# The first weight blocks of v and the second token tile: one load each instead of two

## The chip, the cores and the metric

The kernel runs on one NeuronCore of one Trainium2 chip. The metric is device time in microseconds (us), the median over several executions. An execution that is taken by the hardware profiler gives the trace and the page of the profile; it has a time of its own.

A core has five engines that run side by side, each through its own list of instructions in order: PE (TensorE, matrix products), DVE (VectorE), ACT (ScalarE), POOL (GpSimd) and SP (SyncE, which here only issues transfers). Transfers between HBM and the core's own memory run on 16 DMA engines, which take what SP and ACT issue.

## The reference

One layer of a bidirectional encoder on 1024 tokens of width 1024, all in float32:

```python
h = layer_norm(x, emb_ln_g, emb_ln_b)               # embedding LayerNorm
proj = h @ w_in                                     # 1024 x 5120
q, k, v, z_a, u, z_b, g_a, g_b = split(proj)        # widths 512 x6, 1024 x2
attn = neighbourhood_attention(q, k, v, rpb)        # 8 heads x 64, 8x16 window on a 16x64 grid
y_a = attn * silu(z_a)
u = centred_depthwise_conv(u, conv_w, conv_b)
h2 = rg_lru(u, forward) + rg_lru(u, backward)       # scans along the sequence
y_b = h2 * silu(z_b)
m = sigmoid(g_a + b0) * (y_a @ w_ba) + sigmoid(g_b + b1) * (y_b @ w_bb)
out = layer_norm(ALPHA * h + m @ w_out, ln_g, ln_b)
```

The part that the change touches is the very start: the embedding LayerNorm of the first tokens, and v = h @ w_v, where w_v is 1024 x 512.

## The kernel before

**Tiles.** The 1024 tokens are eight tiles x0 to x7 of 128 tokens x 1024 values (512 KB each). A tile is normalised with the tokens on the 128 partitions, then PE turns it around in two halves of 512 features (`turn(i, kk)`), since a product needs the features on the partitions. w_v is cut into eight blocks k = 0 to 7 of 128 x 512 (256 KB each); they lie in HBM in four pairs c = 0 to 3, and in a pair the two blocks of a partition are side by side, 4 KB in all.

**High and low parts.** For float32 accuracy each operand is split into a rounded high part and a low part (the value less its high part), and a product is three matmuls: high x high, low x high, high x low. For a weight block, ACT makes the high part (`wv_hi(k)`, line 203) and POOL then the low part (`wv_lo(k)`, line 206, recorded at the helper's line 134). For a turned half tile ACT makes the high part (line 368; for the first half of x0 line 514) and DVE the low one (also line 134). `v_part(i, kind, ks)` (line 413) issues the matmuls of tile i: kind "h" needs the high parts of the blocks ks, "a" the low part of the tokens, "w" the low part of the weights.

**The order.** What each engine does, and in which order, is written out by hand from line 487 on, and each engine goes through its list in order. At the start:

- SP issues x0 (two halves), block 0, block 1, pair 1, x1 (two halves), pairs 2 and 3, x2, the first weights of q, x3, x4, some small values, xt4, and then stores the normalised x0 to HBM (`keep(0)`, line 270). Pairs 0 and 1 go to the tile `wvsh`, pairs 2 and 3 to `wvsl`.
- ACT: root for x0, high parts of blocks 0 and 1, high part of the first turned half of x0 (line 514), high parts of blocks 2 and 3, of the second turned half (line 368), of blocks 4 and 5, root for x1 (line 236), high parts of blocks 6 and 7, and so on.
- POOL: the low parts of blocks 0 to 7, one after the other.
- DVE: statistics of x0 and its normalisation, low part of its first turned half, statistics of x1 (line 230, two instructions, one for each half), low part of the second turned half of x0, normalisation of x1 (lines 251, 244 to 246, 254).
- PE: warm-up products on zeros, spreading of gain and bias, first half of x0 turned (line 359), v of x0 with blocks 0 and 1, second half of x0 turned, then the rest of v of x0 as the blocks come, x1 turned, v of x1, and so on. A matmul of v that needs block 4 is the first that needs pair 2.

**Counters of the loads.** Each transfer is booked on one of eight counters, DMAHW0 to DMAHW7, in turn. A transfer is issued only when the transfer eight places before it, which used the same counter, has landed.

**Later.** The token tile x5 uses the memory of x0, so its load waits until the store of x0 has landed; in the same way x6 waits for the store of x1. Around 30 us the results v of the first tiles are stored (`v_d`, line 427), and the buffer `vs` of such a result is written again (line 420) only when the store has landed. At 47.67 us PE spreads the statistics of x7 (`bcp`, line 323), which takes what ACT and DVE have done until then.

Of the kernel before, what the change touches and what calls it, by code (L numbers as in the profile page):

```python
# [72 lines left out]
def encoder_kernel(ctx, tc, x, xt, gb1, gb, w_qk, w_v, w_s, w_ba, w_bb, w_gate, smalls, bias, w_out, out):  # L73
    nc = tc.nc
    V, A, G, PE, SP = nc.vector, nc.scalar, nc.gpsimd, nc.tensor, nc.sync
# [86 lines left out]
    wvs = [hts[0].tile([P, 4, HALF], F32, tag="ht4" + c, name=f"wvs{c}") for c in "hl"]  # L162
# [25 lines left out]

    def load_x(i):
        xs[i] = ln.tile([P, D], F32, tag="x", bufs=5, name=f"x{i}")  # L190
        if i < 2:
            for sl in halves:
                SP.dma_start(xs[i][:, sl], x[i][:, sl])
        else:
            SP.dma_start(xs[i][:], x[i])

    def load_wv(c):
        for part in ((0,), (1,)) if c == 0 else ((0, 1),):
            k = 2 * (c % 2) + part[0]
            SP.dma_start(wvs[c // 2][:, k:k + len(part), :], w_v[c][:, part[0]:part[-1] + 1])  # L200

    def wv_hi(k):
        A.copy(wv[0][k][:], wvs[k // 4][:, k % 4, :])  # L203
# [282 lines left out]

    A.dma_start(gb_row[:], gb1.rearrange("o z (r f) -> (o z r) f", f=P))
    load_x(0)
    load_wv(0)
    load_wv(1)  # L490
    load_x(1)
    load_wv(2)
    load_wv(3)
    load_x(2)
    qk_load(0)
    load_x(3)
# [665 lines left out]
    for slot in range(7 * N_PAIR + 4):  # L1162
        p, k = divmod(slot, 7)
# [184 lines left out]
    for unit in range(-NT, H * NT + PV_LAG):  # L1348
        h, c = divmod(unit, NT)
# [538 lines left out]
```

## Time and profile before

| what | value |
|---|---|
| median of 3 runs | 657.51 us (657.47 to 657.64) |
| profiled execution: its time | 658.84 us |
| profiled execution: its span, first to last instruction | 657.1 us |
| PE busy | 644.1 us, 98% of the span |
| DVE, ACT, POOL busy | 540.6, 413.5, 399.2 us |
| transfers | 118.66 MB, 181 GB/s in the mean |

The span is what the page describes; 1.7 us of the profiled execution's time lie outside it, and it is 1.3 us longer than the median of the plain runs. In the views, a line of the timeline gives start, duration, engine, line of the kernel, operation and what is written and read; in brackets stands how long the engine was idle before, and what ended that. "SPq" is SP's issue of a transfer, and the time beside it is that of issuing, not of moving the data. L140, L134 and the like are lines of the kernel; a helper's line stands for all its callers.

### The profile page before, as it was taken

The page shows a single profiled execution, that of the slowest core. Times are in us where ns is not written, and L with a number is a line of the kernel's source. Part 1 is how long each engine was busy: PE and PEld are TensorE (multiplying, and loading weights), DVE is VectorE, ACT ScalarE, POOL GpSimd, SP SyncE. Part 2 cuts the span into 40 slices and gives each one's busy share as a digit, 9 for nine tenths or more (in the row PEclk, how much of TensorE's full clock was granted, in tenths as well). Part 3 has the DMA queues.
Part 4 walks back from the last instruction along what each step waited for, and adds up shares of the span by engine and source line. Part 5 has one row for each costly group of instructions (what it writes and reads, how often), then busy time and mean ns, then how long its engine had stood idle before and what let it go on. Part 6 is the DMA issues. An engine that isn't in the chain of part 4 may idle for free.

```text
span 657.1 us, 9482 instructions
## 1 busy us (share of the span) xinstructions
PE 644.1 (98%) x3089; PEld 539.4 (82%) x3089; DVE 540.6 (82%) x849; ACT 413.5 (63%) x738; POOL 399.2 (61%) x326
## 2 busy tenths in 40 slices
PE   7999999999999999999999999999999999999994
PEld 6888888888878888888888888889888888888884
DVE  7988998995999799979988695277887875994776
ACT  5569554567776677777666745277777744574253
POOL 5559769933655576558556434012652649989957
PEclk9999999999999999999999999999999999999998
DMA  8674676433333233532362548797977288333033
GB/s 327 218 288 149 197 238 252 145 128 113 128 102 118 87 113 119 170 113 80 135 217 67 186 174 303 280 351 261 359 277 244 66 314 291 111 116 129 17 112 129
DMA packets 54065, 118.66 MB, mean 181 GB/s; under 512 B 5680, under 2 KB 10368, under 8 KB 52480
## 3 DMA queue, kind: packets, MB, share of 16 engines
q1 hardware_dynamic: 53696, 117.67, 51.9%
q8 instruction: 24, 0.39, 0.2%
q10 hardware_dynamic: 320, 0.40, 0.2%
q14 instruction: 25, 0.20, 0.1%
HBM read 82.36 MB, written 35.68 MB: 180 GB/s over the span
## 4 chain that ended last, share of the span: by engine, by line
PE 86%; DVE 6%; DMA 3%; ACT 2%; issue 1%; SPq 0%; DVEq 0%; ACTq 0%
PE a L140 32%; PE mb L140 13%; PE s L140 12%; PE x L140 6%; PE w L140 5%; PE v L413 4%; PE acc L1267 3%; PE s L1219 3%; PE pt L1241 3%; PE g L885 2%; PE q L140 2%; DMA v_d<-vs 1%; DMA wvsl<-in_w_v_dram 1%; DVE uc L843 1%; DVE ws_l L134 1%
## 5 line engine op out<-in xcount | busy, mean ns | idle before, releaser
L140 PE MATMUL a<-ht_h,ws_h 128*128 128x512 f32 x136 | 53.0, 389 | 0.0
L140 PE MATMUL a<-ht_h,ws_l 128*128 128x512 f32 x136 | 52.9, 389 | 0.0
L140 PE MATMUL a<-b_h,wa_h 128*128 128x512 f32 x136 | 52.9, 389 | 0.0
L140 PE MATMUL a<-b_h,wa_l 128*128 128x512 f32 x136 | 52.9, 389 | 0.0
L140 PE MATMUL a<-ht_l,ws_h 128*128 128x512 f32 x136 | 52.9, 389 | 0.0
L140 PE MATMUL a<-b_l,wa_h 128*128 128x512 f32 x136 | 52.9, 389 | 0.0
L1229 DVE CUSTOM_DVE_ANT_0 sc<-s,bias 128x384 f32<-128x384 f32 (+1 forms) x64 | 33.4, 522 | 19.8 <-PE s L1219 9.8
L1248 ACT CAST pt_h<-pt 128x384 fp32r<-128x384 f32 x64 | 29.0, 453 | 23.1 <-PE pt L1241 18.9
L993 POOL CAST wb_h<-wb 128x512 fp32r<-128x512 f32 x9 | 7.0, 781 | 58.3 <-DMA wb<-in_w_bb_dram 37.4
L1234 ACT ACTIVATE p<-sc,summ 128x384 f32<-128x384 f32 (+1 forms) x64 | 37.8, 591 | 5.5 <-DVE summ L1229 5.2
L140 PE MATMUL mb<-ya,wb_h 128*128 128x512 f32 x128 | 39.6, 389 | 0.0
L134 DVE TENSOR_TENSOR pt_l<-pt,pt_h 128x384 fp32r<-128x384 f32 x64 | 33.2, 519 | 1.8 <-ACT pt_h L1248 1.5
L413 PE MATMUL v<-wv,b_h 128*128 128x512 f32 x128 | 32.7, 397 | 1.1 <-ACT wv L203 0.7
L1219 PE MATMUL s<-ks,qs 128*128 128x384 f32 (+1 forms) x128 | 31.7, 329 | 0.0
L1642 POOL TENSOR_TENSOR z<-z,gb 128x512 f32<-128x512 f32 (+1 forms) x22 | 25.9, 1189 | 9.0 <-ACT z L1637 8.2
L1241 PEld LDWEIGHTS pt<-ident,p 128*128 128x128 f32 x176 | 22.9, 140 | 8.9 <-issue 0.9
L140 PEld LDWEIGHTS a<-ht_h,ws_h 128*128 128x128 f32 x136 | 25.5, 188 | 5.5 <-issue 0.2
L140 PEld LDWEIGHTS a<-ht_l,ws_h 128*128 128x128 f32 x136 | 25.5, 188 | 5.3
L140 PEld LDWEIGHTS a<-b_l,wa_h 128*128 128x128 f32 x136 | 25.5, 188 | 5.3
L140 PEld LDWEIGHTS a<-b_h,wa_l 128*128 128x128 f32 x136 | 25.5, 188 | 5.3
L140 PEld LDWEIGHTS a<-b_h,wa_h 128*128 128x128 f32 x136 | 25.5, 188 | 5.3
L140 PEld LDWEIGHTS a<-ht_h,ws_l 128*128 128x128 f32 x136 | 25.5, 188 | 5.2
(579 smaller groups left out, 2296.6 us busy)
## 6 DMA issues: line engine op xcount, KB each, us to landing
ks<-k_d SPq DMA_DIRECT2D x8, 1024.0 KB, 7.5
v_d<-vs SPq DMA_DIRECT2D x8, 512.0 KB, 3.3
q_d<-q SPq DMA_DIRECT2D x8, 512.0 KB, 3.0
ga_d<-ga SPq DMA_DIRECT2D x16, 256.0 KB, 2.0
gb_d<-gb SPq DMA_DIRECT2D x16, 256.0 KB, 2.7
k_d<-k SPq DMA_DIRECT2D x8, 512.0 KB, 3.5
qs<-q_d SPq DMA_DIRECT2D x8, 512.0 KB, 6.0
g<-gb_d SPq DMA_DIRECT2D x16, 256.0 KB, 6.1
```

The source lines that it names most:

```text
L134: eng.tensor_tensor(lo, full, hi.bitcast(F32), ALU.subtract)
L140: PE.matmul(o, a, b, start=first and i == 0, stop=last and i == len(prods) - 1, skip_group_check=not (first and last))
L413: PE.matmul(vos[i][:], a, wv[kind == "w"][k][:], start=vn[i] == 0, stop=vn[i] == 23)
L885: PE.matmul(o[:, n, :], w[:, 2 * d + b, :], us[b][:, n * HALF:(n + 1) * HALF], start=z == 0, stop=z == 1)
L993: G.tensor_copy(hi[:], st[:])
L1219: PE.matmul(o[:, :P * len(near(t))], q[:, t * P:(t + 1) * P], k[:, z, keys], start=z == 0, stop=z == 1)
L1229: V.tensor_tensor_reduce(s[:, :w], o[:, :w], heads[h][2][:, b0:b0 + w], -1.0, 3.0e38, ALU.add, ALU.min, accum_out=sums[h][0][:, t:t + 1])
L1234: A.activation(probs[h % 2][t][:], scs.pop((h, t))[:, :w], AF.Exp, bias=sums[h][0][:, t:t + 1], scale=-1.0, accum_out=sums[h][1][:, t:t + 1])
L1241: PE.transpose(tp[:, n * P:(n + 1) * P], probs[h % 2][t][:, z * P:(z + 1) * P], ident[:])
L1248: A.copy(pt[0][:, span(b)], tps[h, b][:, :P * len(near(b))])
L1267: PE.matmul(acc[n][:, lo - n * HALF:hi - n * HALF], vvs[h // 2][:, b, h % 2, :], pt[:, a:a + hi - lo], start=b in (1, 6) and z == 0, stop= ...
L1642: G.tensor_tensor(z, z, gbs[c, n][:, part], (ALU.mult, ALU.add)[c])
```

## The change

The two loads of pair 0 (blocks 0 and 1) become one of 512 KB, as those of the other pairs are, and x1 is loaded whole, as x2 to x7 are. x0 still comes in two halves. Nothing else is changed.

```diff
     def load_x(i):
         xs[i] = ln.tile([P, D], F32, tag="x", bufs=5, name=f"x{i}")
-        if i < 2:
+        if i < 1:
             for sl in halves:
                 SP.dma_start(xs[i][:, sl], x[i][:, sl])
         else:
             SP.dma_start(xs[i][:], x[i])
 
     def load_wv(c):
-        for part in ((0,), (1,)) if c == 0 else ((0, 1),):
-            k = 2 * (c % 2) + part[0]
-            SP.dma_start(wvs[c // 2][:, k:k + len(part), :], w_v[c][:, part[0]:part[-1] + 1])
+        SP.dma_start(wvs[c // 2][:, 2 * (c % 2):2 * (c % 2) + 2, :], w_v[c])
```

The lists of PE, DVE, ACT and POOL keep their instructions and their order. Two places show what differs. First the start of SP's list, with what each transfer waits for (`x_164` is x0, `x_170` x1, `x_175` x2, `wqk_s` the first weights of q, `x_179` x3, `x_181` x4). Before:

```order
L193 DMA x_164<-in_x_dram 128x512 x2
L200 DMA wvsh<-in_w_v_dram 128x512 x2
L200 DMA wvsh<-in_w_v_dram 128x1024
L193 DMA x_170<-in_x_dram 128x512 x2
L200 DMA wvsl<-in_w_v_dram 128x1024 [waits DMAHW0_49]
L200 DMA wvsl<-in_w_v_dram 128x1024 [waits DMAHW1_49]
L195 DMA x_175<-in_x_dram 128x1024 [waits DMAHW2_49]
L173 DMA wqk_s<-in_w_qk_dram 128x1024 [waits DMAHW3_49]
L195 DMA x_179<-in_x_dram 128x1024 [waits DMAHW4_49]
L195 DMA x_181<-in_x_dram 128x1024 [waits DMAHW5_49]
L498 DMA sm<-in_smalls_dram 128x76 [waits DMAHW6_49]
L307 DMA xt_184<-in_xt_dram 128x1024 [waits DMAHW7_49]
```

And with the change (all lines after the two functions are two less; `x_169` is x1, `x_173` x2, `x_177` x3, `x_179` x4):

```order
L193 DMA x_164<-in_x_dram 128x512 x2
L198 DMA wvsh<-in_w_v_dram 128x1024 x2
L195 DMA x_169<-in_x_dram 128x1024
L198 DMA wvsl<-in_w_v_dram 128x1024 x2
L195 DMA x_173<-in_x_dram 128x1024 [waits DMAHW0_49]
L173 DMA wqk_s<-in_w_qk_dram 128x1024 [waits DMAHW1_49]
L195 DMA x_177<-in_x_dram 128x1024 [waits DMAHW2_49]
L195 DMA x_179<-in_x_dram 128x1024 [waits DMAHW3_49]
L496 DMA sm<-in_smalls_dram 128x76 [waits DMAHW4_49]
L305 DMA xt_182<-in_xt_dram 128x1024 [waits DMAHW5_49]
```

There are two transfers fewer, and from x2 to x4 each one waits for a transfer that stands earlier in the list than before: x3 waited for block 1 (the fourth transfer on SP) and now waits for the second half of x0. Pairs 2 and 3 wait for nothing now. The small values (`sm`) waited for the first half of x1 and now wait for pair 1; xt4 waits for all of x1 in both.

Second, ACT's list around the first weight blocks (`wv_132` and `wv_133` are the high parts of blocks 0 and 1). Before:

```order
L236 ACTIVATE ln0e<-ln0m,few 128x1 [waits DVE_49]
L203 CAST wv_132<-wvsh 128x512 [waits DMAHW3_49]
L203 CAST wv_133<-wvsh 128x512 [waits DMAHW4_49]
L514 CAST b_h<-tp_0_241 128x2x128 [waits PE_49]
L514 CAST b_h<-tp_0_241 128x2x128
L203 CAST wv_134<-wvsh 128x512 [waits DMAHW5_49]
```

And with the change:

```order
L234 ACTIVATE ln0e<-ln0m,few 128x1 [waits DVE_49]
L201 CAST wv_132<-wvsh 128x512 [waits DMAHW3_49]
L201 CAST wv_133<-wvsh 128x512
L512 CAST b_h<-tp_0_239 128x2x128 [waits PE_49]
L512 CAST b_h<-tp_0_239 128x2x128
L201 CAST wv_134<-wvsh 128x512 [waits DMAHW4_49]
```

The cast of block 1 no longer waits for a transfer of its own: that of block 0 now waits for both blocks.

## The prediction

> **What bounds the kernel now.** The waits of PE come first, since PE is busy for 644.1 of the 657.1 us: what does not change when PE waits, or for how long, cannot move the end. In the view of who waited for whom, PE alone, over the whole span, four rows stand out (us in total, times, longest):
>
> ```profile
> PE tp L359 <- DVE x L254: 1.0, 1, 1.0
> PE v L413 <- ACT wv L203: 0.7, 1, 0.7
> PE a L140 <- DVE c L776: 0.7, 1, 0.7
> PE bcp L323 <- DVE t L387: 0.3, 1, 0.3
> ```
>
> The first is PE before it turns x0, ahead of anything that the change touches; the second is PE waiting for weight block 4; the third lies far behind the change, the fourth at 47.67 us. The chain of work that ended last, in order of time (start, us, what), says where the second and the fourth come from:
>
> ```profile
> 4.01 7.74 DMA wvsl<-in_w_v_dram
> ...
> 11.78 0.63 ACT wv L203
> ...
> 12.45 2.42 PE v L413 x9
> ...
> 29.52 8.77 DMA v_d<-vs
> ...
> 38.36 0.06 ACT vs L420
> ...
> 47.67 0.41 PE bcp L323 x2
> ```
>
> Pair 2 lands at 11.75, ACT makes block 4, PE goes on at 12.45. At 47.67 PE waits for a chain that comes from transfers (the store of v, landed at 38.3). So two streams set the end: PE's own, and that of the transfers, which meets PE at 47.67 with 0.34 us to spare on PE's side. Neither touches the first two blocks or x1 directly; the question is what their loads push.
>
> SP's issues (start, us of issuing; "x3" means three in a row) give the landings too, since a transfer waits for the one eight places before it:
>
> ```profile
> 1.65 1.37 SPq L200 DMA_DIRECT2D wvsh<-in_w_v_dram  x3
> 3.06 0.91 SPq L193 DMA_DIRECT2D x<-in_x_dram  x2
> ...
> 7.56 1.92 SPq L195 DMA_DIRECT2D x<-in_x_dram  x2
> ...
> 10.48 0.33 SPq L307 DMA_DIRECT2D xt<-in_xt_dram  x1
> 11.83 0.33 SPq L270 DMA_DIRECT2D h_d<-x  x1
> 21.33 0.33 SPq L195 DMA_DIRECT2D x<-in_x_dram  x1
> ```
>
> At 7.56 x3 goes out as block 1 has landed, at 10.48 xt4 as the second half of x1 has, at 11.83 the store of x0 as pair 2 has, and at 21.33 x5 as that store has. The queue of the DMA engines is full meanwhile, as the rows of the transfers below show (100.3% and 102.3% of 16 engines): what lands when is set by the bytes ahead, not by the time of issue.
>
> **Part 1: cost of a packet.** The rows of queue 1 (packets, MB, share of 16 engines), first for 2.4 to 3.4 us, where nearly all packets are rows of 2 KB, then for 11 to 13 us, where they are of 4 KB:
>
> ```profile
> q1 hardware_dynamic: 203, 0.38, 100.3%
> ...
> q1 hardware_dynamic: 227, 0.83, 102.3%
> ```
>
> That is 1.003 x 16 / 0.38 = 42.2 engine-us for a MB, against 2 x 1.023 x 16 / 0.83 = 39.4. The change turns pair 0 and x1, 1.05 MB, from 2 KB to 4 KB rows: 1.05 x 2.8 / 16 = 0.18 us less for the queue, 0.09 of it by the end of pair 0. All that lands behind x1 comes 0.18 earlier: pair 2 (11.57), the store of x0, and with it x5 and the chain to 47.67. The two issues that go away (0.43 each, 1.37 / 3 less the gaps) are worth nothing beside that: the full queue hides them. Without that cover they would be worth up to 0.9.
>
> The Trainium skill has a price of its own ("DMA: Bandwidth & Descriptors", section "Why small descriptors are slow (HBM only)"): some 3 cycles for a packet beside its beats of 32 bytes. By it 2 KB rows would cost 67 beats and two of them 134 against 131, 2.2% instead of the rows' 7%, and the saving would be an estimated 0.06 us instead of 0.18; the rows are this kernel's, so they stand.
>
> **Part 2: blocks 0 and 1 land together.** ACT's rows:
>
> ```profile
> 5.71 0.62 ACT L203 CAST wv<-wvsh 128x512 fp32r<-128x512 f32 x1 [0.24 <-DMA wvsh<-in_w_v_dram]
> 7.57 0.62 ACT L203 CAST wv<-wvsh 128x512 fp32r<-128x512 f32 x1 [1.25 <-DMA wvsh<-in_w_v_dram]
> 8.21 0.65 ACT L514 CAST b_h<-tp 128x256 fp32r<-128x256 f32 x2
> 9.16 1.14 ACT L203 CAST wv<-wvsh 128x512 fp32r<-128x512 f32 x2 [0.30 <-DMA wvsh<-in_w_v_dram]
> 10.21 0.58 ACT L368 CAST b_h<-tp 128x512 fp32r<-128x512 f32 x1
> 11.78 1.14 ACT L203 CAST wv<-wvsl 128x512 fp32r<-128x512 f32 x2 [0.99 <-DMA wvsl<-in_w_v_dram]
> 12.82 0.29 ACT L236 ACTIVATE ln1e<-ln1m,few 128x1 f32<-128x1 f32 x1
> ```
>
> Block 0 was there at 5.7, block 1 at 7.55. The single load is there when the last byte is, at 7.57 - 0.09 = 7.48. Then ACT casts both (1.14, as the pair at 9.16 took) until 8.62, and the high part of x0's first half begins at 8.64 instead of 8.21: 0.43 late. PE's rows:
>
> ```profile
> 8.64 0.96 PE L413 MATMUL v<-wv,b_h 128*128 128x512 f32 x3 [0.35 <-ACT b_h L514]
> ...
> 11.32 0.40 PE L413 MATMUL v<-wv,b_l 128*128 128x512 f32 x1
> 12.45 1.02 PE L413 MATMUL v<-wv,b_h 128*128 128x512 f32 x3 [0.73 <-ACT wv L203]
> ...
> 14.80 0.63 PE L359 MATMUL tp<-ident,x 128*128 128x128 f32 x4
> ...
> 15.49 1.80 PE L413 MATMUL v<-wv,b_h 128*128 128x512 f32 x6
> ...
> 47.67 0.29 PE L323 MATMUL bcp<-ident,ln7m 128*128 128x128 f32 x1 [0.34 <-DVE t L387]
> ```
>
> The matmuls from 8.64 on go 0.43 later, and so does all of PE until the one at 11.32, which now ends at 12.15. Then PE waited 0.73 for block 4. With pair 2 at 11.57, block 4 is cast by 12.22 (ACT is free: its cast of 10.21, 0.43 later, ends at 11.2), and PE goes on at 12.27 instead of 12.45. So the 0.43 vanish in the 0.73, and **PE gains 0.18 here**. Without that cover the step would cost 0.43.
>
> POOL's rows, the low parts of the blocks:
>
> ```profile
> 6.41 1.27 POOL L134 TENSOR_TENSOR wv<-wvsh,wv 128x512 fp32r<-128x512 f32 x1 [5.12 <-ACT wv L203]
> 8.26 1.29 POOL L134 TENSOR_TENSOR wv<-wvsh,wv 128x512 fp32r<-128x512 f32 x1 [0.59 <-ACT wv L203]
> ...
> 12.47 5.06 POOL L134 TENSOR_TENSOR wv<-wvsl,wv 128x512 fp32r<-128x512 f32 x4
> ```
>
> POOL begins 0.08 after block 0 is cast: at 7.48 + 0.62 + 0.08 = 8.18 instead of 6.41. It then works without a gap, six lows of 1.28 until 15.86 (before: 12.47 + 2 x 1.27 = 15.0). The sixth is block 5, and PE asks for it in the second matmul of the six from 15.49, about 0.28 later: 15.77, and 15.98 with part 3. It fits by 0.12. Blocks 6 and 7 are wanted later still.
>
> **Part 3: x1 lands whole.** DVE's rows:
>
> ```profile
> 9.82 1.36 DVE L230 BATCH_NORM_STATS2 ln1t<-x 128x6 f32<-128x512 f32 x2 [0.24 <-DMA x<-in_x_dram]
> ...
> 13.14 0.16 DVE L244 RECIPROCAL ln1e<-ln1e 128x1 f32<-128x1 f32 x1 [0.27 <-ACT ln1e L236]
> ...
> 13.90 0.75 DVE L254 SCALAR_TENSOR_TENSOR x<-x,ln1e,gps 128x512 f32<-128x512 f32 x1
> ```
>
> The statistics began with the first half at 9.82; the whole tile is there at 10.48 - 0.18 = 10.30, so DVE is 0.48 late. It then waited 0.27 for ACT's root (12.82), which takes that much back: 0.21 stay. x1's first half is normalised at 13.90 + 0.75 + 0.21 = 14.86, and PE, which turns it at 14.80 (0.15 behind DVE), does so at 15.01. **PE's stream is 0.21 late from here**, whatever it gained at 12.27, and has no wait until 47.67.
>
> **The sum.** PE would be ready for `bcp` at 47.67 - 0.34 + 0.21 = 47.54, the transfers' chain at 47.67 - 0.18 = 47.49. The later of the two counts: 0.13 before today. Behind it everything moves along. Against the profiled span: 657.1 - 0.13. The profiled execution (658.84) lies 1.3 above the median, so the shift goes on the median: 657.51 - 0.13, **657.4 us**. The unknown is when pair 0 lands: not before 5.7, when its first half did, and not later than the row that is like it, pair 1, also 512 KB: begun at 2.59 (the third of the three issues from 1.65), cast at 9.16, so 6.6 us, which gives 8.25 here. I take 7.48, near the landing of the same bytes.
>
> **The rivals.** With about 0.2% (1.3 us) as the least that a measurement of this kernel tells from no change, nearly all of them end within it.
>
> A. The forecast. Its own range is 657.1 to 657.8, the ends being no saving in packets and 0.3 more delay, or 0.34 at 47.67 won whole.
>
> B. POOL's lows become the bound, and it is slower. For it: POOL has no gap left after the change. Against: 0.12 us to spare. It decides when pair 0 lands after 7.73 (0.12 until PE waits for block 5, 0.13 more until PE passes the old 47.67). At the upper bound, 8.25, the lows begin at 8.95, block 5 is done at 16.63, 0.65 after its place; PE is 0.21 + 0.65 late, reaches `bcp` at 48.19, 0.52 after today: 658.0.
>
> C. The early dips of the transfers go with the small rows. The first two rows of the windows (length, busy us of PE, PEld, DVE, ACT, POOL, then granted clock, DMA share, GB/s) show them, the third is for E:
>
> ```profile
> 3.50:4.00 0.50, 0.34 (x4) 0.34 (x4) 0.50 (x1) 0.11 (x1) 0.00 (x0) 1.00 0.88 209
> 4.00:4.50 0.50, 0.50 (x6) 0.50 (x4) 0.45 (x2) 0.00 (x0) 0.00 (x0) 1.00 0.70 205
> ...
> 654.00:655.00 1.00, 0.00 (x0) 0.00 (x0) 0.00 (x0) 0.00 (x0) 0.00 (x0) 0.50 1.03 358
> ```
>
> Over that 1 us the engines moved 0.17 MB less than at 380 GB/s, some 0.43 us of work. Were it saved, all landings came 0.61 earlier; x1 at 9.87, which makes part 3 nearly nothing, and PE, held by its own work until 12.15, gains at most 0.3, and the 0.34 at 47.67: together 0.6, 656.9. Against: nothing shows that the dips come from the rows' size.
>
> D. The merged load is cut into the same rows, so nothing is saved and only the later start stays: PE is 0.21 + 0.18 late, 0.05 past the 0.34: 657.6. Against: pair 1 has the same form and moves in 4 KB.
>
> E. PE's clock falls in the gap that grows. The last row above shows that it can, to 0.50, with PE idle; in the others it is 1.00, with PE at 0.34 of 0.50. PE's gap before the first v matmul grows from 0.35 to 0.78. Some 3.4 us at half speed, the time from 8.6 to 12, would cost 1.7: 659.2. Against: PE is idle for longer in today's start (1.00 before the first turn) and keeps 1.00. The Trainium skill ("TensorE: Matmul & The Clock Gate", section "Part 1: The HAM clock gate (the "warmup" mystery)") says that the clock halves after an idle window of about 3.4 us; no gap here comes near that, which agrees.
>
> **How the numbers follow.** A 0.62, B 0.17, C 0.10, D 0.06, E 0.03, something unseen 0.02. The range runs from C to a little past B: 656.8 to 658.2; E and the unseen are left out. Faster by over 0.2% asks for more than C gives: 0.02. Slower by over 0.2% is E, and a part of the unseen: 0.05. No change: 0.93.
>
> **What would show it.** Casts of blocks 0 and 1 back to back from about 7.5; the first v matmul at 9.1; pair 2's first cast near 11.6 and PE on at 12.3; x1's statistics at 10.3 and its first turn at 15.0; POOL without a gap from 8.2; at 47.5 PE's wait before `bcp` nearly gone. If the casts begin past 7.7 and PE waits for POOL near 16, B holds; if pair 2 is there by 11.2, C; a granted clock under 1.00 before 20 us is E. A time outside the range with none of these would mean that something far behind the loads has moved.

## The result, and the profile after

| | median | lowest to highest | executions |
|---|---|---|---|
| before, on the same chip | 657.59 us | 657.36 to 658.02 | 22 |
| with the change | 658.54 us | 657.65 to 659.66 | 22 |

The ratio is 1.0014 [1.0007, 1.0020]: the change makes the kernel 0.95 us slower. That is 0.14%, inside the 0.2% called "no change", but 0.34 us above the top of the predicted range, and on the other side of the forecast. The single executions also lie further apart (2.0 us, against 0.7).

The profiled execution of the change took 658.91 us, with a span of 657.1, the same span as that of before in the prediction. The two can't be set side by side: that of before (658.84) lies 1.3 above its median of 657.51, that of the change 0.37. So an unchanged copy of before was profiled once more (called the copy below; 657.93 us, 0.42 above its own median, span 656.1). It stands for before in what follows, and its line numbers are those of before, two above those of the change.

Three of the waits of PE in the change:

```profile
PE v L411 <- ACT b_h L512: 0.9, 1, 0.9
PE a L140 <- DVE c L774: 0.7, 1, 0.7
PE tp L357 <- DVE x L252: 0.4, 1, 0.4
```

PE's wait before `bcp`, 0.3 in the prediction, is gone, and so is that for block 4. The last row is PE before it turns x0 (0.9 in the copy). The wait before the first v matmul has grown to 0.9. ACT's timeline shows why, first the change, then the copy:

```profile
5.47 0.29 ACT L234 ACTIVATE ln0e<-ln0m,few 128x1 f32<-128x1 f32 x1 [1.75 <-DVE ln0m L229]
8.05 1.14 ACT L201 CAST wv<-wvsh 128x512 fp32r<-128x512 f32 x2 [2.29 <-DMA wvsh<-in_w_v_dram]
...
11.91 1.14 ACT L201 CAST wv<-wvsl 128x512 fp32r<-128x512 f32 x2 [0.27 <-DMA wvsl<-in_w_v_dram]
```

```profile
5.07 0.29 ACT L236 ACTIVATE ln0e<-ln0m,few 128x1 f32<-128x1 f32 x1 [1.48 <-DVE ln0m L231]
5.72 0.62 ACT L203 CAST wv<-wvsh 128x512 fp32r<-128x512 f32 x1 [0.35 <-DMA wvsh<-in_w_v_dram]
7.58 0.62 ACT L203 CAST wv<-wvsh 128x512 fp32r<-128x512 f32 x1 [1.24 <-DMA wvsh<-in_w_v_dram]
...
11.48 1.14 ACT L203 CAST wv<-wvsl 128x512 fp32r<-128x512 f32 x2 [0.89 <-DMA wvsl<-in_w_v_dram]
```

Three things are late, not one. Pair 0 is there at 8.05, 0.47 later than the second block alone was. The root for x0 starts at 5.47 instead of 5.07, so x0, which is loaded ahead of pair 0, has become later too. And pair 2, loaded behind, comes at 11.91 instead of 11.48, not earlier. PE's timeline, the change and the copy:

```profile
9.51 1.07 PE L411 MATMUL v<-wv,b_h 128*128 128x512 f32 x3 [0.92 <-ACT b_h L512]
...
12.59 1.02 PE L411 MATMUL v<-wv,b_h 128*128 128x512 f32 x3
...
15.12 0.63 PE L357 MATMUL tp<-ident,x 128*128 128x128 f32 x4
...
15.82 1.95 PE L411 MATMUL v<-wv,b_h 128*128 128x512 f32 x6
17.61 0.60 PE L357 MATMUL tp<-ident,x 128*128 128x128 f32 x4
...
47.65 0.27 PE L321 MATMUL bcp<-ident,ln7m 128*128 128x128 f32 x1
```

```profile
8.55 0.98 PE L413 MATMUL v<-wv,b_h 128*128 128x512 f32 x3 [0.35 <-ACT b_h L514]
...
12.15 1.02 PE L413 MATMUL v<-wv,b_h 128*128 128x512 f32 x3 [0.57 <-ACT wv L203]
...
14.51 0.63 PE L359 MATMUL tp<-ident,x 128*128 128x128 f32 x4
...
15.20 1.80 PE L413 MATMUL v<-wv,b_h 128*128 128x512 f32 x6
16.84 0.60 PE L359 MATMUL tp<-ident,x 128*128 128x128 f32 x4
...
46.88 0.27 PE L323 MATMUL bcp<-ident,ln7m 128*128 128x128 f32 x1
```

PE is 0.96 late at its first v matmul, 0.44 after the place where the copy waits for block 4, 0.61 when it turns the first half of x1, 0.77 when it turns the second, and still 0.77 at `bcp`. No wait at `bcp` takes anything back, in either of the two. The step from 0.44 to 0.61 is DVE, which normalises the first half of x1 0.66 later (its last step begins at 14.27, in the copy at 13.61). The last 0.15 is POOL: the six matmuls take 1.95 instead of 1.80. POOL's timeline in the change, and in the copy, and the chain that ended last in the change:

```profile
8.75 5.03 POOL L134 TENSOR_TENSOR wv<-wvsh,wv 128x512 fp32r<-128x512 f32 x4 [7.47 <-ACT wv L201]
13.75 5.04 POOL L134 TENSOR_TENSOR wv<-wvsl,wv 128x512 fp32r<-128x512 f32 x4
```

```profile
6.42 1.26 POOL L134 TENSOR_TENSOR wv<-wvsh,wv 128x512 fp32r<-128x512 f32 x1 [5.13 <-ACT wv L203]
```

```profile
1.64 6.39 DMA wvsh<-in_w_v_dram
...
8.05 0.63 ACT wv L201
...
13.75 2.55 POOL wv L134 x2
...
16.34 1.43 PE v L411 x5
17.77 0.44 PE tp L357 x4
```

POOL begins at 8.75 instead of 6.42 and works without a gap; the sixth low part is done at 16.30, and PE takes it at 16.34. In this execution the chain that ended last runs from the load of pair 0 through seven and a half microseconds of POOL into PE.

### The profile page after: what moved, and what is told of

Read it like the earlier page. It is cut to its first block, busy times and chain, and to the rows that moved or that the text cites. A ratio compares the mean times of both kernels' runs of the same rounds, so it can differ in the third digit from the quotient of the medians.

```text
span 657.1 us, 9480 instructions
## 1 busy us (share of the span) xinstructions
PE 644.7 (98%) x3089; PEld 540.1 (82%) x3089; DVE 540.7 (82%) x849; ACT 413.5 (63%) x738; POOL 398.6 (61%) x326
## 4 chain that ended last, share of the span: by engine, by line
PE 91%; DVE 5%; issue 1%; DMA 1%; POOL 1%; ACT 0%; SPq 0%; DVEq 0%; ACTq 0%
PE a L140 32%; PE mb L140 13%; PE s L140 12%; PE v L411 6%; PE x L140 6%; PE w L140 5%; PE acc L1265 3%; PE q L140 3%; PE s L1217 3%; PE pt L1239 3%; PE g L883 2%; DMA wvsh<-in_w_v_dram 1%; DVE uc L841 1%; POOL wv L134 1%; DVE ws_l L134 1%
```

## The experiments

"Before" in a ratio is the unchanged kernel, timed beside each run on the same chip; its medians were 657.48 to 657.57. The runs were on four chips, so two versions are best compared by their ratios. A difference of less than about 0.1% lies inside most intervals. All profiles are single executions.

### Which half of the change costs it

**The copy** has no edit.

> The kernel before, unchanged, measured as any other kernel here. Theory N (the 0.95 us between the medians, 657.59 and 658.54, is how executions of one program scatter): 658.2 to 658.9, so about 0.1% over its own runs. Theories P and X (the change costs time): 657.4 to 657.9, a ratio within 0.03% of 1.

Measured: 657.51 us, ratio 1.0001 [0.9992, 1.0010].

**Only pair 0 in one load:**

```diff
     def load_wv(c):
-        for part in ((0,), (1,)) if c == 0 else ((0, 1),):
-            k = 2 * (c % 2) + part[0]
-            SP.dma_start(wvs[c // 2][:, k:k + len(part), :], w_v[c][:, part[0]:part[-1] + 1])
+        SP.dma_start(wvs[c // 2][:, 2 * (c % 2):2 * (c % 2) + 2, :], w_v[c])
```

> Only the two loads of blocks 0 and 1 become one; x1 still comes in halves. Theory P (the late landing of blocks 0 and 1 makes POOL's chain of low parts the bound, and PE waits for it near 16 us): nearly all of the cost, 658.2 to 658.6, POOL without a gap from 8.7 us on and PE waiting for POOL's lows. Theory X (the whole x1 makes DVE late): 657.4 to 657.8. Theory N: no difference from the unchanged copy.

Measured: 658.52 us, 1.0015 [1.0006, 1.0024]. In its profile PE waits for block 4 again, so pair 2, later by 0.67 than in the copy, is what holds PE there, and not POOL. PE stays 0.67 late until it has turned x1 (17.51 against 16.84), so in this execution POOL adds nothing:

```profile
7.87 1.14 ACT L201 CAST wv<-wvsh 128x512 fp32r<-128x512 f32 x2 [1.95 <-DMA wvsh<-in_w_v_dram]
...
12.15 1.14 ACT L201 CAST wv<-wvsl 128x512 fp32r<-128x512 f32 x2 [0.69 <-DMA wvsl<-in_w_v_dram]
```

**Only x1 whole:**

```diff
-        if i < 2:
+        if i < 1:
```

> Only x1 is loaded whole; blocks 0 and 1 still come one by one. Theory P: 657.4 to 657.8, DVE some 0.2 to 0.4 us later at x1's normalisation, hidden at 47.67 us. Theory X: 658.2 to 658.6. Theory N: no difference from the unchanged copy.

Measured: 657.55 us, 1.0002 [0.9993, 1.0011].

The cost is that of pair 0; x1 in one load costs nothing that can be measured. In the profile with x1 whole PE does not wait for block 4 either:

```profile
11.40 0.86 PE L413 MATMUL v<-wv,b_h 128*128 128x512 f32 x3
...
16.22 0.60 PE L359 MATMUL tp<-ident,x 128*128 128x128 f32 x4
```

The wait for block 4, in which the prediction hid the later start, was 0.73 and 0.57 in two profiles of before. It is gone here because pair 2 came earlier: its first cast began at 10.47, against 11.48 in the copy.

**The change, with the low part of block 1 on DVE**, to shorten POOL's list by one:

```diff
-    def wv_lo(k):
-        lo_of(G, wv[1][k][:], wvs[k // 4][:, k % 4, :], wv[0][k][:])
+    def wv_lo(k, eng=G):
+        lo_of(eng, wv[1][k][:], wvs[k // 4][:, k % 4, :], wv[0][k][:])
...
+    wv_lo(1, V)
     turn_lo(0, 0)
...
-    for k in KS[1:]:
+    for k in KS[2:]:
```

> The changed kernel, with the low part of block 1 made by DVE (0.7 us, where DVE waited 0.49 us for ACT in the changed kernel) instead of POOL (1.26 us). Theory P: POOL's lows of blocks 2 to 7 end 1.2 us earlier, PE's waits for POOL near 16 us go, and the time falls back to 657.5 to 657.9. Theory X: DVE is fuller, so 658.5 to 658.8. Theory N: no difference from the unchanged copy.

Measured: 658.44 us, 1.0013 [1.0004, 1.0022], as slow as the change. PE's rows show that this did not separate anything:

```profile
15.53 0.63 PE L357 MATMUL tp<-ident,x 128*128 128x128 f32 x4 [0.48 <-issue]
...
16.22 1.80 PE L411 MATMUL v<-wv,b_h 128*128 128x512 f32 x6
```

POOL was relieved (the six matmuls take 1.80 again), but the low part took DVE 1.35 us, not the 0.7 expected, and DVE, which normalises x1, became late in its place: the last step of x1's first half begins at 14.68 instead of 14.27, and PE turns it 0.41 later than in the change. Another way of relieving POOL was needed; it comes below.

### One load, or late blocks, or the size of the rows

**Both blocks cast only when both are there**, with the loads of before (ACT casts block 1 first, which waits for the second load):

```diff
-    wv_hi(0)
     wv_hi(1)
+    wv_hi(0)
```

> The kernel before, its loads untouched; only ACT casts block 1 first and then block 0, so that block 0 is cast no earlier than with the single load (ends near 8.8 us). Theory C (the cost is the late cast of block 0 and what hangs on it, PE's first v matmuls and POOL's lows): 658.2 to 658.7. Theory T (the 4 KB rows of pair 0, right behind x0, slow the DMA engines, and all loads behind land later): 657.4 to 657.9. Theory I (one issue less lets SP issue the later loads earlier, and the queue of some engines fills up): 657.4 to 657.9.

Measured: 658.39 us, 1.0011 [1.0002, 1.0020]. A late cast costs 0.82 us by the medians, with the loads of before. POOL's and PE's timelines of its profile:

```profile
8.13 5.04 POOL L134 TENSOR_TENSOR wv<-wvsh,wv 128x512 fp32r<-128x512 f32 x4 [6.85 <-ACT wv L203]
13.13 5.05 POOL L134 TENSOR_TENSOR wv<-wvsl,wv 128x512 fp32r<-128x512 f32 x4
```

```profile
15.74 1.43 PE L413 MATMUL v<-wv,b_h 128*128 128x512 f32 x5 [0.41 <-POOL wv L134]
```

PE now waits for the sixth low part, as the rival on POOL (B) says. The edit overstates it: block 0 is cast second here, so POOL starts one cast (0.6) later than in the change for the same landing.

**Pair 0 in one load, but in rows of 2 KB** (the two blocks of each of pairs 0 and 1 lie apart in `wvsh`, so that a row of 4 KB in HBM becomes two pieces; here and below the diffs show the line of the load alone, and `wv_hi` and `wv_lo` read the blocks where they lie):

```diff
-            SP.dma_start(wvs[c // 2][:, k:k + len(part), :], w_v[c][:, part[0]:part[-1] + 1])
+        SP.dma_start(wvs[0][:, c::2, :] if c < 2 else wvs[1][:, 2 * (c % 2):2 * (c % 2) + 2, :], w_v[c])
```

> Pair 0 in one load as in the change, x1 in halves, but the blocks of pairs 0 and 1 lie apart in the tile, so that the rows of both loads are of 2 KB. Theory C: 658.2 to 658.7. Theory T: 657.4 to 658.0, x0's second half landing near 4.1 us and pair 2 near 11.6 again. Theory I: 658.2 to 658.7.

Measured: 657.54 us, 1.0000 [0.9992, 1.0009]: one load costs nothing when its rows are short. ACT's row:

```profile
6.12 1.14 ACT L204 CAST wv<-wvsh 128x512 fp32r<-128x512 f32 x2 [0.62 <-DMA wvsh<-in_w_v_dram]
```

Both blocks are there at 6.12, 1.9 us before those of the change.

**Pair 0 in two loads again, but each with 64 partitions and rows of 4 KB:**

```diff
+        for rows in (slice(0, 64), slice(64, P)) if c == 0 else (slice(0, P),):
+            SP.dma_start(wvs[c // 2][rows, 2 * (c % 2):2 * (c % 2) + 2, :], w_v[c][rows])
```

> Pair 0 in two loads again, but cut by partitions (64 each), so that the rows are of 4 KB and block 0 still needs both loads; x1 in halves. Theory C: 658.2 to 658.7. Theory T: 658.2 to 658.7, x0's second half landing at 4.4 us or later. Theory I: 657.4 to 657.9.

Measured: 658.13 us, 1.0015 [1.0002, 1.0028]; one of the eleven executions took 662.76 and raises the ratio, and by the medians the cost is 0.56 us. Two loads with rows of 4 KB cost, one load with rows of 2 KB doesn't, so the number of loads is not the cause. The cut by partitions is a change of its own, and what it does alone was not measured.

**Pair 0 in one load, and the small values (`sm`) loaded right behind it,** ahead of pair 1:

```diff
     load_wv(0)
+    SP.dma_start(sm[:], smalls)
     load_wv(1)
```

> Pair 0 in one load with 4 KB rows, x1 in halves; the load of the small values (38 KB) is moved up right behind pair 0, so that SP has as many issues as before and the later loads go out when they did and wait for the same places in the list. Theory C: 658.2 to 658.8. Theory T: 658.2 to 658.8. Theory I: 657.4 to 657.9.

Measured: 657.78 us, 1.0006 [0.9997, 1.0015]: most of the cost goes away by the median; the interval still holds no change and 0.15%. This is what the rival on the issues (I) expected. But that rival also expected a cost of the single load with rows of 2 KB, which has one issue less too (657.54), and none of the two loads with rows of 4 KB (658.13). Alone it does not hold.

### Which rows matter

**2 KB rows in pair 0 alone** (pair 1 keeps its 4 KB):

```diff
+        SP.dma_start((wvs[0][:, 0::3, :], wvs[0][:, 1:3, :])[c] if c < 2 else wvs[1][:, 2 * (c % 2):2 * (c % 2) + 2, :], w_v[c])
```

> Pair 0 in one load with rows of 2 KB, pair 1 with its rows of 4 KB as before, x1 in halves. Theory R (the 4 KB rows of pair 0 make it land near 7.9 us instead of 6.1 to 7.5): 657.4 to 657.8, casts of blocks 0 and 1 from 6.1 to 7.2. Theory R1 (the rows of pair 1 matter, since they are what stands behind pair 0): 658.2 to 658.6. Theory J (nothing but the joint wait for both blocks counts, whatever the rows): 658.2 to 658.6.

Measured: 657.43 us, 1.0000 [0.9991, 1.0009]. The same single load of pair 0 with rows of 4 KB had cost 1 us; nothing else differs but the place of the blocks in `wvsh`. Its profiled execution is a long one (658.36), and there ACT and PE show that short rows do not always bring pair 0 early, and that PE can then wait for POOL:

```profile
7.51 1.14 ACT L204 CAST wv<-wvsh 128x512 fp32r<-128x512 f32 x2 [2.08 <-DMA wvsh<-in_w_v_dram]
```

```profile
15.79 1.43 PE L414 MATMUL v<-wv,b_h 128*128 128x512 f32 x5 [0.28 <-POOL wv L134]
```

**2 KB rows in pair 1 alone**, pair 0 in one load with 4 KB:

```diff
+        SP.dma_start((wvs[0][:, 1:3, :], wvs[0][:, 0::3, :])[c] if c < 2 else wvs[1][:, 2 * (c % 2):2 * (c % 2) + 2, :], w_v[c])
```

> The counterpart: pair 0 in one load with rows of 4 KB, pair 1 with rows of 2 KB, x1 in halves. Theory R: 658.2 to 658.6, casts of blocks 0 and 1 from about 7.9. Theory R1: 657.4 to 657.8. Theory J: 658.2 to 658.6.

Measured: 657.68 us, 1.0004 [0.9995, 1.0013]: most of the cost is gone here too, by the median. The theory of pair 0's rows alone (R) had expected 658.2 to 658.6 here, that of pair 1's rows alone (R1) the same in the run before; each missed once, and short rows in either pair seem to be enough.

**The whole change, with 2 KB rows in pairs 0 and 1:**

```diff
-        if i < 2:
+        if i < 1:
...
+        SP.dma_start(wvs[0][:, c::2, :] if c < 2 else wvs[1][:, 2 * (c % 2):2 * (c % 2) + 2, :], w_v[c])
```

> The whole change (single loads of pair 0 and of x1), but pairs 0 and 1 with rows of 2 KB. Theory R: 657.4 to 657.8, so the change costs nothing once its rows stay small. Theory R1: the same. Theory J: 658.2 to 658.7.

Measured: 658.05 us, 1.0007 [0.9999, 1.0016], with executions from 657.48 to 659.11 that spread between. Inconclusive: it lies between what R and R1 expected and what J did. (J expected a cost from the joint wait for both blocks, whatever the rows.) In its profile (658.97) pair 0 is there only at 7.74.

The windows from 2 to 6 us (length, busy us of PE, PEld, DVE, ACT, POOL, granted clock, DMA share, GB/s) set the two kinds of rows side by side. First the copy and the change:

```profile
2.00:6.00 4.00, 3.74 (x30) 3.50 (x29) 2.49 (x7) 1.40 (x5) 0.00 (x0) 1.00 0.94 292
```

```profile
2.00:6.00 4.00, 3.61 (x25) 3.36 (x24) 2.12 (x5) 1.12 (x4) 0.00 (x0) 1.00 0.88 246
```

Then pair 0 alone in one load; the same with rows of 2 KB in pair 0; and with rows of 2 KB in pair 1:

```profile
2.00:6.00 4.00, 3.67 (x25) 3.43 (x24) 1.97 (x5) 1.12 (x4) 0.00 (x0) 1.00 0.75 243
```

```profile
2.00:6.00 4.00, 3.74 (x32) 3.36 (x30) 2.44 (x6) 1.12 (x4) 0.00 (x0) 1.00 0.87 301
```

```profile
2.00:6.00 4.00, 3.74 (x31) 3.51 (x30) 1.92 (x5) 1.12 (x4) 0.00 (x0) 1.00 0.86 294
```

All eighteen profiles of this study fall into two groups in these 4 us, with nothing between:

| the loads right behind x0 | profiles | GB/s from 2 to 6 us |
|---|---|---|
| pairs 0 and 1 both in rows of 4 KB, one after the other (change, pair 0 alone, both with DVE's low part, pair 0 without that low part, two loads of 64 partitions) | 6 | 235 to 268 |
| all others, those with the small values between the pairs and with 4 KB in one of the pairs among them | 12 | 292 to 318 |

All six of the first group are slower than before, by ratios of 1.0011 to 1.0017; of the others only the late cast is clearly slower, for another reason, and perhaps the whole change with rows of 2 KB. So what goes with the cost is rows of 4 KB behind rows of 4 KB at the very start, whichever load they come in. The grouping was made with the profiles at hand. The rate does not set the landing of pair 0 by itself: in the long executions above it came at 7.51 and 7.74 with 301 and 305 GB/s. The copy moves 46 GB/s x 4 us = 0.18 MB more than the change; at the 418 GB/s that the change's engines move later this is an estimated 0.44 us of work, about what x0 (0.40), pair 0 (0.47) and pair 2 (0.43) were late by:

```profile
8.00:12.00 4.00, 3.08 (x18) 2.35 (x18) 3.20 (x6) 3.40 (x8) 3.25 (x3) 1.00 1.03 418
```

### Is it POOL?

**Pair 0 in one load, and the low part of block 1 on DVE:** the edit to `load_wv` of the kernel with pair 0 alone, and

```diff
+    wv_lo(1, V)
...
-    for k in KS[1:]:
+    for k in KS[2:]:
```

> Pair 0 in one load with rows of 4 KB, x1 in halves, and the low part of block 1 on DVE, so that POOL is ahead by 1.2 us. Theory B (POOL's chain of lows is what turns the late landing into time): 657.6 to 658.0. If instead the late landings of pairs 0 and 2 themselves hold PE (its first v matmul near 9.3, block 4 near 12.8): 658.3 to 658.7.

Measured: 658.79 us, 1.0017 [1.0008, 1.0026], above what either theory expected. DVE is in the way again, and PE waits for it before it turns x1:

```profile
15.16 0.63 PE L357 MATMUL tp<-ident,x 128*128 128x128 f32 x4 [0.30 <-DVE x L252]
```

It says nothing on POOL. So in the next three the low part of block 1 is left out, and PE multiplies by the high part of that block in its place: as many matmuls, but not the right v.

**Before, without the low part of block 1:**

```diff
-            PE.matmul(vos[i][:], a, wv[kind == "w"][k][:], start=vn[i] == 0, stop=vn[i] == 23)
+            PE.matmul(vos[i][:], a, wv[kind == "w" and k != 1][k][:], start=vn[i] == 0, stop=vn[i] == 23)
...
-    for k in KS[1:]:
+    for k in KS[2:]:
```

> The kernel before, with the low part of block 1 left out (POOL makes seven lows instead of eight, and PE uses the high part of block 1 in its place, so v is wrong by that product; the number of matmuls is the same). The control for the next two: POOL has room in the kernel before, so 657.3 to 657.7 under both theories B and L.

Measured: 657.36 us, 0.9999 [0.9991, 1.0008]: in before POOL's list costs nothing that can be measured.

**The late cast, without that low part:** both edits, this one and

```diff
-    wv_hi(0)
     wv_hi(1)
+    wv_hi(0)
```

> Loads untouched, ACT casts block 1 before block 0 (658.39 before), and the low part of block 1 left out as in the control. Theory B (POOL's chain of lows makes the price): back to 657.4 to 657.8, no wait of PE for POOL near 15.7 us. Theory L (ACT and PE are held by the landings and the late cast itself): 658.1 to 658.6.

Measured: 657.60 us, 1.0003 [0.9994, 1.0011], against 658.39 with it. PE goes through the six matmuls without a wait:

```profile
14.74 1.80 PE L413 MATMUL v<-wv,b_h 128*128 128x512 f32 x6
```

So what a late cast costs, it costs through POOL's list, as the two profiles show; by the times alone it is less sure, since the two intervals overlap.

**Pair 0 in one load, without that low part:** the edit above to the matmul and the loop, and

```diff
+        SP.dma_start(wvs[c // 2][:, 2 * (c % 2):2 * (c % 2) + 2, :], w_v[c])
```

> Pair 0 in one load of 4 KB rows, x1 in halves (658.52 before), and the low part of block 1 left out as in the control. Theory B: 657.5 to 657.9. Theory L: 658.2 to 658.7, PE waiting for block 4 near 12.5 us or for the first v matmul.

Measured: 658.09 us, 1.0011 [1.0002, 1.0020], against 658.52 with it: some 0.4 us come back by the medians (0.3 by the ratios), and 0.6 stay (their intervals overlap, so this split is rough). In its profile PE waits for DVE twice, the longer time before it turns x0 (1.6, against 0.9 in the copy), and ACT's root for x0 says since when DVE is late:

```profile
PE tp L357 <- DVE x L252: 1.9, 2, 1.6
```

```profile
6.01 0.29 ACT L234 ACTIVATE ln0e<-ln0m,few 128x1 f32<-128x1 f32 x1 [2.45 <-DVE ln0m L229]
```

The statistics of x0 have ended late (6.01 against 5.07), since its second half landed late, and with them the whole chain of the normalisation: the second half of x1 is turned at 17.21, 0.37 later than in the copy. That part POOL has nothing to do with.

### Does an early landing win anything?

**All four pairs in one load each, with rows of 2 KB**, x1 in halves:

```diff
+        SP.dma_start(wvs[c // 2][:, c % 2::2, :], w_v[c])
```

> All four pairs in one load each with rows of 2 KB, x1 in halves. If small rows keep the early landings together, 657.2 to 657.5, no worse than the kernel before; if it is only pair 0 that counts, 657.4 to 657.7, as with pairs 0 and 1; if 2 KB rows cost 7% more of the queue's time everywhere, 657.6 to 657.9.

Measured: 657.38 us, 1.0006 [0.9995, 1.0016] (one of twelve executions took 661.36): no version here is clearly faster than before. In its profile the other stream shows:

```profile
PE bcp L324 <- DVE t L388: 0.9, 1, 0.9
```

The transfers' chain can be the last to arrive at `bcp`, then; it is in some executions and not in others.

## Why the prediction was wrong

Two steps of the forecast failed. It took 0.34 us off PE's lateness for a wait at `bcp` that neither the copy nor the change has; and it let pair 0 land at 7.48 and pair 2 at 11.57, where the change's casts of them began at 8.05 and 11.91. The second weighs more: with PE 0.77 late, as in the change's profile, the time would have come out longer even with the cushion of 0.34.

| profile of | x1's second half turned, us | span, us | difference | PE's wait at `bcp` |
|---|---|---|---|---|
| copy | 16.84 | 656.1 | 639.3 | none |
| x1 whole | 16.22 | 655.5 | 639.3 | none |
| pair 0 in one load | 17.51 | 656.7 | 639.2 | none |
| change | 17.61 | 657.1 | 639.5 | none |
| before (in the prediction) | 17.13 | 657.1 | 639.9 | 0.3 |
| all pairs in 2 KB rows | 16.77 | 657.4 | 640.6 | 0.9 |

(The differences are taken before rounding.)

**The cushion: wrong.** That the stream of the transfers "meets PE at 47.67 with 0.34 us to spare on PE's side" was true of one execution. In the copy, in the change and in both halves of the change PE has no wait there, and the end follows the turn of x1 by 639.2 to 639.5 us: whatever PE loses at the start stays lost. This was the term that turned +0.21 on PE's side into -0.13 in the sum. With the forecast's own terms and no cushion the answer would have been +0.21. That has the right sign by luck: it is the price of x1 in one load, which the runs do not show.

**The base: wrong.** "The profiled execution (658.84) lies 1.3 above the median, so the shift goes on the median" took it for granted that an execution at the median has the same waits. The copy's profile is 1.0 shorter with the same program: 0.29 of that had gathered when x1 was turned, 0.34 is the wait at `bcp`, and the rest was not located. The cushion belongs to that execution. The cover for block 4 (0.73) is there in the copy too, as 0.57, and did its work: of the 0.96 by which the change's first v matmul is late, 0.44 are left behind it. But the forecast had only 0.43 to hide, and a gain of 0.18 left over.

**Part 1, the price of a packet: measured in one place, wrong where it was used.** The price of rows of 4 KB was read at 11 to 13 us, that of rows of 2 KB at 2.4 to 3.4, so the two differ in time as well as in size. In the first microseconds they made the engines move less, not more, so neither "all that lands behind x1 comes 0.18 earlier" (pair 2: 11.91 against 11.48) nor the landing of pair 0 at 7.48 (8.05; 7.87 with pair 0 alone) held, and x0, which had been left out of the account, came 0.4 later. The bound of 8.25 held the landing; the value chosen was 0.57 too early. The Trainium skill ("Perfetto Trace Analysis", section "DMA Optimizations") has both sides: its first point advises to batch small transfers into larger ones, from 2 KB to 4 KB or 8 KB for instance, and its second says that splitting transfers into smaller chunks may let some start sooner. Here the second agrees with the traces as far as block 0 goes (5.72 in two loads, 8.05 for the pair in one), and the first, taken for the rows of these first loads, does not: with two pairs of 4 KB rows behind x0, 246 GB/s from 2 to 6 us against 292.

**Part 2, ACT and POOL: right in kind.** The casts are back to back, POOL has no gap, and the sixth low part is what PE takes last; the start of POOL was put at 8.18 and was 8.75. The 0.12 to spare was read from the long execution too: PE is at the six matmuls at 15.20 in the copy, not at 15.49, and by that place the sixth low part (15.86) would have been 0.17 too late (15.20 + 0.28 + 0.21 = 15.69) even with pair 0 at 7.48. The profile of pair 0 in rows of 2 KB shows this: casts from 7.51, and PE waits for POOL. With pair 0 past 7.73, the condition of rival B was met, and PE did take the sixth low part the moment it was done. B's price of +0.5 (658.0) had the 0.34 taken off; without it, 0.21 + 0.65 is 0.86, and the medians say 0.95. That is near by luck: it stands for a landing at 8.25, and in the change's profile POOL costs only 0.15, since PE comes 0.62 late to the six matmuls anyway. B is not the whole cause: without the low part of block 1, and so with a shorter list on POOL, 0.6 of the 1.0 stayed.

**Part 3, x1 whole: not borne out.** Alone it costs nothing (1.0002 [0.9993, 1.0011]); the 0.21 could not be told from that. In its profile the statistics of x1 began at 9.40, against 9.54 in the copy, and the second half of x1 was turned 0.62 earlier. In the change they began at 10.63 (10.30 was said), but there DVE was late already: its low part before them began at 9.77, against 8.80 in the copy.

**The other rivals.** C, that the dips of the transfers go: the opposite, they became deeper (246 GB/s against 292). D, that the rows are not merged: the same load with 4 KB and with 2 KB rows differs by 1 us, and from 2 to 6 us the change moved 0.98 MB in 401 packets, the copy 1.16 MB in 585, so the size of the rows did change. E, the clock: it is 1.00 in every window of the change's first 60 us; not seen.

**What stays open.** Why the DMA engines move less when rows of 4 KB follow each other directly behind x0. That it takes both pairs is seen in the rates (304 and 294 GB/s with the small values between, or with 2 KB in pair 1); in the times it rests on two medians (657.78 and 657.68) whose intervals reach to the cost itself. How the 0.95 divides between POOL and the later landings is not settled: the profiles give POOL 0.15 (the change) and nothing (pair 0 alone), the runs without the low part 0.3 to 0.4 with wide intervals. And why the whole change with rows of 2 KB lies between is not known.

## What to carry to other kernels

A wait that is seen in one profile is cover or cushion only if it is there in a second profile of the same program; where the profiled execution is longer than the median, one should ask first which of the waits are that excess. So is a margin: the place that PE had in the long execution made POOL's list fit by 0.12 us. A load that is merged makes its first consumer wait for its last byte, and an engine whose list only just fits (POOL here) can pass that on. The price of a row taken at one time of the kernel need not hold for its first loads: measure there.

## What the hardware showed that was not expected

One load or two is the same (1.0000 [0.9991, 1.0009] with 2 KB rows in pair 0), while the size of the rows of that one load moves the end by 1 us. What goes with it is the rate of the first transfers, 235 to 268 GB/s from 2 to 6 us against 292 to 318, by the size of the rows in two loads that follow each other. It seems to work backwards too: x0, issued ahead, is normalised later, its root starting between 5.06 and 6.01 in the eight profiles with pair 0 in rows of 4 KB, and between 5.03 and 5.21 in the ten others.

A single execution of this kernel can lie 1.3 us above the median of the plain ones (658.84 against 657.51) with nothing changed; the copy's own executions span 657.31 to 658.11, those of pair 0 in one load 657.69 to 659.87. Here the change to the first loads moved the spread as well as the middle.
